# A one-core hybrid decoder layer: first products, broadcasts and gate rows in split passes

## The chip, the cores and the metric

One NeuronCore of a Trainium2 chip runs the whole layer as one program. The metric is device microseconds of one execution, the median of several runs.

## The reference, cut to what matters

One decoder layer over 512 tokens of width 2048, batch 1, float32. `c` gives shift, scale and gate through one matrix; the normed input goes through one wide input projection whose columns feed two head groups.

```
mod = silu(c) @ w_ada + b_ada;  shift, scale, gate = split(mod, 3)
h = rmsnorm(x, ln_g) * (1 + scale) + shift
p = h @ w_in + b_in
y_m = mlstm_group(...)      # 4 heads of 256, causal, chunkwise, gates i and f
y_n = nsa_group(...)        # 16 query heads, 4 groups of keys and values
y = concat(y_m, y_n) @ w_out
out = rmsnorm(x + gate * y, final_g)
```

In the second group, keys and values are also compressed: blocks of 32 tokens, 16 apart (31 blocks, 4 groups), are flattened to 2048 numbers and sent through `gelu(blk @ w1) @ w2` to a key and a value of 64 numbers each. Every query attends to the 31 compressed blocks, to selected blocks and to a window, and the three results are mixed by gates. In the first group the decay between two tokens needs one row per head, `fl - mr` (the running sum of the log forget gate less the running maximum), on all partitions. `gate` multiplies the rows of the output, so each of its 2048 numbers is needed on all partitions too.

## The kernel before, in words

Tokens lie on the free axis (512 columns), features on partitions, until the output projection. Almost every product is made of three TensorE passes on rounded operands (type F32R in the program): high by high, high by low and low by high, where `split` (L119) makes the high part with a copy on ScalarE (L123) and the low part with a subtraction (L126) on VectorE or, in the stretch where `pat` is "p", on GpSimd. `proj(name)` (L279) makes one tile of 128 input-projection columns: two loads of 512 KB into the tag `raw` (three buffers, L111), four quarters each split into tags `whi` and `wlo` (four buffers each), 48 matmuls of 512 columns (L291 to L293).

A few small products are still done on plain F32 operands, and each such call stands in the trace as two matmul records:

- `compress(kv)` (L437): the hidden layer of the compressed blocks, 16 calls for keys and 16 for values, the weights `raw` as the stationary operand and the gathered rows `cst`, read with a step of eight numbers, as the moving one (L444); then gelu and the second matrix.
- `memory_head` (L709): one row on 128 partitions, four partitions deep.
- `gate_columns` (L793): four column sums for each quarter of the gate.
- `chunk_rows` (L838): the gate columns turned to rows on all partitions, one 128-wide call for each.

In `gather` (L539) the weights of the 32 compressed blocks are transposed, split to `ph` and `pl`, and multiplied in two passes with `vcmp` (L548, L549), on 32 partitions; the same function serves the other two branches on 128 partitions.

The program is written in one order; a planner then orders the instructions of each engine by that order and by when buffers and inputs come free in its own reckoning, and gives out the buffers of a tag in the same way. Loads all go through one queue, SP's. Around the change the written order is: the projections kc0, kc1, vc0, then `compress(0)`, vc1, k0 and v0 for the first group, `compress(1)`, then the query tiles.

Of the kernel before, what the change touches and what calls it, by code (L numbers as in the profile page):

```python
# [10 lines left out]
F32 = mybir.dt.float32  # L11
F32R = mybir.dt.float32r
AF = mybir.ActivationFunctionType
# [73 lines left out]
def layer_kernel(ctx: ExitStack, tc: tile.TileContext, x, cols, ada, ada_g, w_ko, w_tiles,  # L87
# [18 lines left out]
    def psb(tag, name):  # L106
        return psum.tile([P, 512], F32, tag=tag, name=name, bufs=PSB[tag])
# [5 lines left out]
    def raw_tile(name):  # L113
        return ws.tile([P, 1024], F32, tag="raw", name=name, bufs=RAW)
# [164 lines left out]
    def proj(name, tag="pj"):  # L279

        ti = TIDX[name] - NKO
        ps = psb(tag, f"pj_{name}")
        for hf in range(2):
            raw = raw_tile(f"w_{name}_{hf}")
            nc.sync.dma_start(raw, w_tiles[ti, hf])
            for q in range(2):
                wh, wl = split(raw[:, q * 512:(q + 1) * 512], 512, f"w_{name}_{hf}{q}")
                for j in range(4):
                    k = hf * 8 + q * 4 + j
                    c = slice(j * P, (j + 1) * P)  # L290
                    pe.matmul(ps, wh[:, c], hhi[k], start=(k == 0), stop=False)  # L291
                    pe.matmul(ps, wh[:, c], hlo[k], start=False, stop=False)  # L292
                    pe.matmul(ps, wl[:, c], hhi[k], start=False, stop=(k == KT - 1))  # L293
# [6 lines left out]
    SIDE = 2  # L300

# [7 lines left out]
    gr = const.tile([P, T], F32, name="gr")  # L309
    kcmp = const.tile([P, NG, 32], F32, name="kcmp")  # L310
    vcmp = const.tile([32, NG, P], F32R, name="vcmp")
# [14 lines left out]
    na = napool.__enter__()  # L326

# [54 lines left out]
    rw = gr[64:68, :]  # L382
# [10 lines left out]
    ve.tensor_sub(rw, fl, mr)  # L393
# [17 lines left out]
    for hd in range(MH):  # L411
# [4 lines left out]
    cst = [[na.tile([P, 1056], F32, tag=("kh", "kl")[vr], name=f"cst{kv}{vr}", bufs=2)[:, :1024]  # L416
            .rearrange("p (g t) -> p g t", g=NG) for vr in range(2)] for kv in range(2)]
    def block_rows(kv, ct2):
        nm = f"{'kv'[kv]}c{ct2}"
        ps = proj(nm)  # L420
        for gg in range(2):
            r = slice(64 * gg, 64 * gg + 64)
            pv = ps[r, :].rearrange("p (b l r) -> p b l r", l=8, r=2)
            for par in range(2):
                for vr in range(2):
                    po = COLS["pos"][0] + ((kv * 2 + par) * 2 + vr) * 8
                    ve.scalar_tensor_tensor(
                        cst[kv][vr][64 * par:64 * par + 64, 2 * ct2 + gg, :]
                        .rearrange("p (b l) -> p b l", l=8),
                        pv[:, :, :, par], bcol(nm)[r, :],  # L430
                        ct[r, po:po + 8].unsqueeze(1).to_broadcast([64, 32, 8]),
                        op0=ALU.add, op1=ALU.add)

    gp.memset(kcmp, 0.0)
    ve.tensor_copy(vcmp.rearrange("p g c -> p (g c)"),
                   zero[0:32, 0:1].to_broadcast([32, NG * P]))
    def compress(kv):  # L437

        hid = psb("ms", f"hid{kv}")
        for half in range(2):  # L440
            raw = raw_tile(f"w1_{kv}{half}")
# [6 lines left out]
        hs = na.tile([P, NG * NCMP], F32, tag="hs", name=f"hs{kv}", bufs=1)  # L448
        sc.activation(hs, hid[:, 0:NG * NCMP], AF.Gelu_apprx_tanh)
        if kv == 0:  # L450
            kc = psb("ms", "kcps")
            pe.matmul(kc[:, 0:NG * NCMP], w2s[:, 0:128], hs, start=True, stop=True)
            ve.tensor_copy(kcmp[:, :, 0:NCMP],
                           kc[:, 0:NG * NCMP].rearrange("p (g b) -> p g b", b=NCMP))
        else:
            vc = psb("ms", "vcps")
            for g in range(NG):
                pe.matmul(vc[0:NCMP, g * DH:(g + 1) * DH], hs[:, g * NCMP:(g + 1) * NCMP],
                          w2s[:, 128:192], start=True, stop=True)
            vv = vc[0:NCMP, 0:NG * DH].rearrange("p (g d) -> p g d", d=DH)  # L460
            sc.copy(vcmp[0:NCMP, :, 0:DH], vv)
            ve.tensor_sub(vcmp[0:NCMP, :, DH:P], vv, vcmp[0:NCMP, :, 0:DH].bitcast(F32))

    block_rows(0, 0)
    block_rows(0, 1)
    block_rows(1, 0)
    compress(0)
    block_rows(1, 1)

    def kv_prep(g):  # L470
        kh = na.tile([P, 1056], F32R, tag="kh", name=f"kh{g}", bufs=2)
        kl = na.tile([P, 1056], F32R, tag="kl", name=f"kl{g}", bufs=2)
        sc.copy(kh[:, 0:32], kcmp[:, g, :])
        ve.tensor_sub(kl[:, 0:32], kcmp[:, g, :], kh[:, 0:32].bitcast(F32))
        ps = proj(f"k{g}")
# [23 lines left out]
    def attend(g, qs, kh, kl, vt):  # L499
# [6 lines left out]
        for i in reversed(range(NT)):  # L506
# [32 lines left out]
            def gather(srcs, rows, vmat, last, nme):  # L539

                tp = psb("tp", f"tp{nme}")
                for hd in range(HPG):
                    pe.transpose(tp[0:rows, hd * P:(hd + 1) * P], srcs[hd], ident)  # L543
                ph = na.tile([P, T], F32R, tag="ph", name=f"ph{nme}", bufs=2)
                pl = na.tile([P, T], F32R, tag="pl", name=f"pl{nme}", bufs=2)
# [63 lines left out]
    def state(g):  # L609
        kv = kv_prep(g)  # L610
        if g == 0:
            compress(1)
        return (q_prep(g), *kv)
# [54 lines left out]
    def memory_head(hd, vh, vl):  # L668
# [39 lines left out]
        dc = COLS["delta"][0] + hd * 16  # L708
        pe.matmul(rb, ct[64:68, dc:dc + 1].to_broadcast([4, P]), rw, start=True, stop=True)  # L709
# [68 lines left out]
    def gate_columns():  # L778
        for n in range(4):
            acc = na.tile([P, T], F32, tag="q", name=f"gacc{n}", bufs=QB)  # L780
            for k in range(KT):
# [12 lines left out]
            ve.tensor_add(gcol[:, 4 * n:4 * n + 4], ps[:, 0:4], col("b_agate", 4 * n, 4))  # L794
# [37 lines left out]
    wl_l = op.tile([P, KT, 256], F32R, name="wl_l")  # L832
    def chunk_rows(n, c0, cn):

        ps = psb("ms", f"gps{n}")
        for j in range(cn // P):
            k = c0 // P + j
            pe.matmul(ps[:, j * P:(j + 1) * P], gcol[:, k:k + 1].to_broadcast([P, P]), ident,  # L838
                      start=True, stop=True)
# [189 lines left out]
```

## Time and profile before

| | |
|---|---|
| median of 3 runs | 1138.44 us (1138.37 to 1139.06) |
| the profiled execution | 1138.83 us, span of its instructions 1137.0 us |
| TensorE matmul busy | 1110.3 us, 98% of the span |
| VectorE, ScalarE, GpSimd busy | 668.1, 546.6, 198.3 us |
| mean granted TensorE clock | 0.996 of full speed |

A matmul's record goes on for a while after the next one has begun, so the cost of one on a busy TensorE is read from its start to the start of the next, not from its length. In a timeline, rows that follow one another with the same operation and operands are merged, with their count behind x.

### The profile page before, as it was taken

Reading aid. Unit: us, or ns where it says so; the run is one execution under the profiler, and the core shown is the slowest. Engines: PE = TensorE matmul, PEld = TensorE weight load, DVE = VectorE, ACT = ScalarE, POOL = GpSimd, SP = SyncE. Lnnn points to the kernel's source line nnn. Section 1 sums busy time; section 2 is a strip of 40 time slices with the busy share of each in tenths; the row PEclk is TensorE's granted clock in tenths of the full one; section 3 lists DMA queues with packets and bytes.
Section 4 is the critical chain, followed back from the end, with each engine's and each line's share of the span. In section 5 each row is a group of like instructions: output and inputs, shape, how many; then the busy total and the mean of one; then the engine's idle time right before and its main releaser. Section 6 shows DMA issues by size and latency. Waiting matters only on the chain.

```text
span 1137.0 us, 18337 instructions
## 1 busy us (share of the span) xinstructions
PE 1110.3 (98%) x6796; PEld 919.1 (81%) x6796; DVE 668.1 (59%) x1712; ACT 546.6 (48%) x1222; POOL 198.3 (17%) x174
## 2 busy tenths in 40 slices
PE   4999999999999999999999999999999999999997
PEld 4777788887887888788788777888888888888896
DVE  5766464216647657666666885578567357334273
ACT  5443452237666758766756734333433354223242
POOL 1000200443335325333533210000000000000000
PEclk9999999999999999999999999999999999999999
DMA  9999423232111211121121442238416222444334
GB/s 378 406 402 363 146 93 130 93 112 74 56 56 59 72 56 56 62 68 57 61 70 57 138 158 77 91 134 290 151 57 214 84 91 75 148 140 133 104 114 158
DMA packets 49338, 150.29 MB, mean 132 GB/s; under 512 B 5856, under 2 KB 7776, under 8 KB 48736
## 3 DMA queue, kind: packets, MB, share of 16 engines
q1 hardware_dynamic: 49248, 149.12, 37.7%
q8 instruction: 53, 0.87, 0.3%
q14 instruction: 37, 0.30, 0.1%
HBM read 144.90 MB, written 4.19 MB: 131 GB/s over the span
## 4 chain that ended last, share of the span: by engine, by line
PE 93%; DVE 2%; DMA 2%; ACT 1%; issue 0%; POOL 0%; SPq 0%; ACTq 0%; POOLq 0%; DVEq 0%
PE ko L256 7%; PE po L899 5%; PE po L900 5%; PE po L901 5%; PE pj_q L291 3%; PE pj_mz L291 3%; PE pj_mx L291 3%; PE pj_mz L292 3%; PE pj_mv L291 3%; PE pj_q L292 3%; PE pj_mz L293 3%; PE pj_q L293 3%; PE pj_mx L292 3%; PE pj_mv L293 3%; PE pj_mv L292 3%; PE pj_mx L293 3%
## 5 line engine op out<-in xcount | busy, mean ns | idle before, releaser
L524 ACT ACTIVATE ep<-ep,nm 128x512 f32<-128x512 f32 (+3 forms) x128 | 71.3, 558 | 19.3 <-DVE nm L517 18.6
L749 POOL TENSOR_TENSOR sm<-sm,mhalf 128x1 f32<-128x1 f32 x16 | 10.1, 640 | 254.5 <-DVE sm L748 113.1
L788 DVE SCALAR_TENSOR_TENSOR gacc<-adag,sil,gacc 128x512 f32<-128x512 f32 x60 | 48.0, 801 | 7.5 <-DMA adag<-in_dram 6.9
L517 DVE CUSTOM_DVE_ANT_0 ep<-ss,bias 128x512 f32<-128x512 f32 (+3 forms) x64 | 30.3, 486 | 30.7 <-PE tps L543 22.1
L517 DVE CUSTOM_DVE_ANT_0 ep<-sw,bias 128x512 f32<-128x512 f32 (+3 forms) x64 | 29.9, 484 | 18.9 <-PE sw L585 12.9
L194 DVE SCALAR_TENSOR_TENSOR acc<-ada,sil,acc 128x256 f32<-128x256 f32 x75 | 35.7, 476 | 1.5
L220 ACT ACTIVATE hhi<-xts,md 128x512 fp32r<-128x512 f32 x16 | 13.1, 817 | 47.3 <-DVE md L210 47.3
L537 DVE TENSOR_SCALAR ep<-ep,ff 128x512 f32<-128x512 f32 (+3 forms) x80 | 33.2, 461 | 0.6
L861 POOL TENSOR_TENSOR rf<-rf,mhalf 128x1 f32<-128x1 f32 x4 | 2.2, 549 | 178.7 <-ACT tz L854 163.1
L547 DVE TENSOR_TENSOR pls<-tps,phs 128x512 fp32r<-128x512 f32 x40 | 27.0, 685 | 10.6 <-ACT phs L546 10.1
L547 DVE TENSOR_TENSOR plw<-tpw,phw 128x512 fp32r<-128x512 f32 x40 | 27.2, 684 | 6.7 <-ACT phw L546 6.1
L504 POOL TENSOR_SCALAR bias<-ct 128x640 f32<-128x640 f32 x16 | 29.4, 1839 | 2.3 <-DVE nm L517 1.2
L546 ACT CAST phw<-tpw 128x512 fp32r<-128x512 f32 x40 | 22.8, 583 | 13.3 <-PE tpw L543 8.4
L524 ACT ACTIVATE ec<-ec,nm 128x32 f32<-128x32 f32 x64 | 20.3, 317 | 17.6 <-DVE nm L517 17.2
L546 ACT CAST phs<-tps 128x512 fp32r<-128x512 f32 x40 | 23.0, 582 | 11.2 <-DVE nm L517 5.0
L203 PEld LDWEIGHTS gp<-ada,cb 128*32 128x32 f32 x1328 | 20.5, 112 | 8.9 <-issue 6.8
L543 PE MATMUL tpw<-ct,ep 128*128 128x128 f32 x160 | 26.8, 273 | 0.1
L517 DVE CUSTOM_DVE_ANT_0 ec<-ss,bias 128x32 f32<-128x32 f32 x48 | 8.9, 187 | 29.1 <-PE ss L575 28.8
L535 ACT ACTIVATE ep<-ep,ff 128x512 f32<-128x512 f32 (+3 forms) x48 | 23.5, 552 | 4.4 <-DVE ff L529 4.3
L232 PE MATMUL xt<-ct,xs 128*128 128x128 f32 x64 | 11.0, 330 | 14.3 <-DVE xs L169 12.4
L203 PE MATMUL gp<-ada,cb 128*32 128x64 f32 x1328 | 24.9, 224 | 0.0
L543 PE MATMUL tps<-ct,ep 128*128 128x128 f32 x160 | 24.8, 272 | 0.0
(1084 smaller groups left out, 3831.4 us busy)
## 6 DMA issues: line engine op xcount, KB each, us to landing
ada<-in_dram SPq DMA_DIRECT2D x64, 512.0 KB, 7.0
adag<-in_dram SPq DMA_DIRECT2D x64, 256.0 KB, 3.7
wo<-in_dram SPq DMA_DIRECT2D x32, 512.0 KB, 3.4
w_q<-in_dram SPq DMA_DIRECT2D x16, 512.0 KB, 3.5
w_mx<-in_dram SPq DMA_DIRECT2D x16, 512.0 KB, 3.4
w_mv<-in_dram SPq DMA_DIRECT2D x16, 512.0 KB, 3.4
w_mz<-in_dram SPq DMA_DIRECT2D x16, 512.0 KB, 3.5
w_mo<-in_dram SPq DMA_DIRECT2D x16, 512.0 KB, 3.4
```

The lines of the kernel that those rows point to most:

```text
L256: pe.matmul(ko_ps[j], (wl if p == 1 else wh)[:, c], (hlo if p == 2 else hhi)[k], start=(k == 0 and p == 0), stop=(k == KT - 1 and p == 2))
L291: pe.matmul(ps, wh[:, c], hhi[k], start=(k == 0), stop=False)
L292: pe.matmul(ps, wh[:, c], hlo[k], start=False, stop=False)
L293: pe.matmul(ps, wl[:, c], hhi[k], start=False, stop=(k == KT - 1))
L517: ve.tensor_tensor_reduce(dst, src, bs, -0.125, 3.0e38, ALU.add, ALU.min, nm[:, c:c + 1])
L524: sc.activation(tiles[hd], tiles[hd], AF.Exp, bias=nm[:, 4 * br + hd:4 * br + hd + 1], scale=-1.0, accum_out=zz[:, 4 * br + hd:4 * br + hd ...
L543: pe.transpose(tp[0:rows, hd * P:(hd + 1) * P], srcs[hd], ident)
L547: ve.tensor_sub(pl[0:rows, :], tp[0:rows, :], ph[0:rows, :].bitcast(F32))
L788: ve.scalar_tensor_tensor(acc, raw, w, acc, op0=ALU.mult, op1=ALU.add)
L899: pe.matmul(pss[i][:, :cn], yh[k][:, t], wh[:, c], start=f0, stop=False)
L900: pe.matmul(pss[i][:, :cn], yh[k][:, t], wl[:, c], start=False, stop=False)
L901: pe.matmul(pss[i][:, :cn], yl[k][:, t], wh[:, c], start=False, stop=l0)
```

## The change

It has five parts.

1. The hidden layer of the compressed blocks: `block_rows` now leaves rounded high and low rows (`csh`, `csl`), `w1` is split as well, into a tile `wt` that takes a buffer of the tag `raw`, and the operands change places: the rows are the stationary operand, the two halves of a weight stand side by side as 256 moving columns. A second call of 128 columns adds the low rows. The result has blocks on partitions, so it is transposed back (`compress_turn`). The steps are hung behind given projections: `turn(0)` behind vc1, the second layer of the keys and the values' hidden layer behind k0, `turn(1)` behind v0, the values' second layer behind the first query tile.
2. The row broadcast in `memory_head`: the row is split into eight partitions (high on four, low on four, carried there by a DMA from SBUF to SBUF) and multiplied in one pass.
3. `gather` for the compressed branch: high and low stand on 64 partitions of one tile, `vcmp` holds its rows twice, and one pass does both.
4. The gate columns: four calls on 32 columns of the array each, then a transpose on VectorE.
5. The gate rows: the columns are split, set on a diagonal by VectorE, and summed by a matrix of ones in two passes as wide as the chunk.

```diff
+        if name in behind:
+            with tc.issue_after(last):
+                behind[name]()
...
-    gr = const.tile([P, T], F32, name="gr")
+    rw = const.tile([8, T], F32R, name="rw")
+    dsel = const.tile([8, 64], F32R, name="dsel")
...
-    ve.tensor_sub(rw, fl, mr)
+    ve.tensor_copy(dsel, ds)
+    ve.tensor_sub(rd, fl, mr)
+    sc.copy(rh, rd)
+    ve.tensor_copy(rs[0:4, :], rh.bitcast(F32))
+    ve.tensor_sub(rd, rd, rh.bitcast(F32))
+    nc.sync.dma_start(rs[4:8, :], rd)
+    sc.copy(rw, rs)
...
+            ch, cl = cst[kv][vr]
+            c = slice(ct2 * 512, (ct2 + 1) * 512)
+            sc.copy(ch[:, c], cf)
+            ve.tensor_sub(cl[:, c], cf, ch[:, c].bitcast(F32))
...
+            def rows(t, l):
+                return t.rearrange("p (b l) -> p b l", l=8)[:, half:half + nb, l]
...
-            for l in range(8):
-                pe.matmul(hid[:, 0:NG * NCMP], raw[:, l * P:(l + 1) * P],
-                          cst[kv][half].rearrange("p g (b l) -> p g b l", l=8)
-                          [:, :, half:half + NCMP, l],
-                          start=(half == 0 and l == 0), stop=(half == 1 and l == 7))
+            for q in range(2):
+                rv = raw[:, q * 512:(q + 1) * 512]
+                wt = ws.tile([P, 2, 512], F32R, tag="raw", name=f"w1s{kv}{half}{q}", bufs=RAW)
+                sc.copy(wt[:, 0], rv)
+                ve.tensor_sub(wt[:, 1], rv, wt[:, 0].bitcast(F32))
+                for j in range(4):
...
+                    pe.matmul(hid[0:nb, 0:256].rearrange("p (v c) -> p v c", v=2), rows(ch, l), wt[:, :, c],
+                              start=f0, stop=False)
+                    pe.matmul(hid[0:nb, 0:P], rows(cl, l), wt[:, 0, c],
+                              start=False, stop=(half == 1 and l == 7))
...
+    def keys():
+        compress(0, hid[0])
+        hid[1] = compress_hidden(1)
+    behind.update(vc1=lambda: turn(0), k0=keys, v0=lambda: turn(1), q0_0=lambda: compress(1, hid[1]))
...
+                if rows == 32:
+                    sc.copy(ph[0:32, :], tp[0:32, :])
+                    ve.tensor_sub(ph[32:64, :], tp[0:32, :], ph[0:32, :].bitcast(F32))
+                    pe.matmul(ops, vmat, ph[0:64, :], start=first[0], stop=last)
...
-        pe.matmul(rb, ct[64:68, dc:dc + 1].to_broadcast([4, P]), rw, start=True, stop=True)
+        pe.matmul(rb, dsel[:, hd * 16:hd * 16 + 1].to_broadcast([8, P]), rw, start=True, stop=True)
...
-            for j in range(4):
-                pe.matmul(ps[:, j:j + 1], acc[:, j * P:(j + 1) * P], ones[:, 0:1], start=True, stop=True)
+            for g in range(4):
+                pe.matmul(ps[32 * g:32 * g + 32, 0:P].rearrange("p (j c) -> p j c", j=4), ones[:, 0:32],
+                          acc.rearrange("p (j c) -> p j c", j=4)[:, :, 32 * g:32 * g + 32],
+                          start=True, stop=True, tile_position=(0, 32 * g))
...
-            pe.matmul(ps[:, j * P:(j + 1) * P], gcol[:, k:k + 1].to_broadcast([P, P]), ident,
-                      start=True, stop=True)
+            dg = op.tile([P, 4, P], F32R, tag="dg", name=f"dg{n}{v}", bufs=2)
...
+            pe.matmul(ps[:, :cn], onr, dg[:, 0:m].rearrange("p a b -> p (a b)"), start=(v == 0), stop=(v == 1))
```

## Rows read from the trace of the kernel before

**Rows 1.** The page, busy time of each engine: us, share of the span, instructions.

```profile
PE 1110.3 (98%) x6796; PEld 919.1 (81%) x6796; DVE 668.1 (59%) x1712; ACT 546.6 (48%) x1222; POOL 198.3 (17%) x174
```

**Rows 2.** The page, shares of the chain that ended last.

```profile
PE 93%; DVE 2%; DMA 2%; ACT 1%; issue 0%; POOL 0%; SPq 0%; ACTq 0%; POOLq 0%; DVEq 0%
```

**Rows 3.** Stretches from:to: length, busy us per engine, granted clock, DMA share, GB/s.

```profile
130.00:262.00 132.00, 132.00 (x594) 109.57 (x594) 44.87 (x96) 49.62 (x82) 33.99 (x28) 1.00 0.31 103
...
637.30:640.70 3.40, 3.40 (x16) 3.10 (x16) 3.40 (x13) 3.40 (x10) 0.00 (x0) 0.50 0.50 169
```

**Rows 4.** Timeline of TensorE around the keys' hidden layer: start, length, operands, count.

```profile
184.98 0.39 PE L293 MATMUL pj_vc<-hhi,w_vc_11l 128*128 128x512 f32 x1
185.21 7.37 PE L444 MATMUL hid<-cst,w 128*128 128x124 f32 x32
192.22 0.60 PE L291 MATMUL pj_vc<-hhi,w_vc_00h 128*128 128x512 f32 x1
```

**Rows 5.** Timeline of TensorE: rounded operands, 128 and 256 moving columns.

```profile
828.16 0.27 PE L723 MATMUL s<-qh,xh 128*128 128x128 f32 x1
828.27 0.27 PE L724 MATMUL s<-ql,xh 128*128 128x128 f32 x1
...
1118.70 0.28 PE L908 MATMUL po<-wl_h,yh 128*128 128x256 f32 x1
1118.82 0.28 PE L909 MATMUL po<-wl_l,yh 128*128 128x256 f32 x1
```

**Rows 6.** Timeline of TensorE: passes on 32 partitions, one alone and a pair.

```profile
277.98 0.50 PE L548 MATMUL o<-phc,vcmp 32*128 32x512 f32 x1
278.40 0.50 PE L292 MATMUL pj_v<-hlo,w_v_10h 128*128 128x512 f32 x1
278.74 0.39 PE L293 MATMUL pj_v<-hhi,w_v_10l 128*128 128x512 f32 x1
...
656.25 0.49 PE L548 MATMUL o<-phc,vcmp 32*128 32x512 f32 x1
656.58 0.39 PE L549 MATMUL o<-plc,vcmp 32*128 32x512 f32 x1
656.90 0.50 PE L548 MATMUL o<-phs,v 128*128 128x512 f32 x1
```

**Rows 7.** Timeline of TensorE: the row broadcast of the first head.

```profile
563.99 1.12 PE L709 MATMUL rb<-gr,ct 4*128 4x512 f32 x2
565.04 0.50 PE L584 MATMUL sw<-kh,q_q 128*128 128x512 f32 x1
```

**Rows 8.** Timeline of TensorE: gate columns, and the sums on 32 columns of the array.

```profile
121.08 0.88 PE L203 MATMUL gp<-ada,cb 128*32 128x64 f32 x48
...
740.21 0.72 PE L793 MATMUL gcps<-ones,gacc 128*128 128x1 f32 x6
```

**Rows 9.** Timeline of TensorE: the gate rows of the first chunk.

```profile
947.10 1.05 PE L838 MATMUL gps<-ct,gcol 128*128 128x128 f32 x8
947.90 0.48 PE L899 MATMUL po<-wo000h,yh 128*128 128x512 f32 x1
```

**Rows 10.** Timeline of SP's queue: loads of `w1` for the keys, then the next projections.

```profile
170.18 1.98 SPq L442 DMA_DIRECT2D w<-in_dram  x2
178.85 5.82 SPq L285 DMA_DIRECT2D w_vc<-in_dram  x2
```

**Rows 11.** Instructions of `split`: length in ns (min/median/max) of copy and subtraction, by engine.

```profile
L123 ACT CAST w_q_00h<-w_q x8: 604/620/620, 220.1 to 431.1; 128x512 fp32r<-128x512 f32 x8
...
L126 DVE TENSOR_TENSOR w_mv_00l<-w_mv,w_mv_00h x6: 673/692/693, 674.7 to 870.2; 128x512 fp32r<-128x512 f32 x6
L126 POOL TENSOR_TENSOR w_k_00l<-w_k,w_k_00h x4: 1292/1296/1297, 195.9 to 378.4; 128x512 fp32r<-128x512 f32 x4
```

**Rows 12.** DMA issues: count, KB each, median us from issue to landing.

```profile
w_vc<-in_dram SPq DMA_DIRECT2D x4, 512.0 KB, 3.4
...
wg<-in_dram SPq DMA_DIRECT2D x4, 128.0 KB, 2.4
```

More of the change, by code (lines that the diff above doesn't have):

```diff
@@ L292, in proj @@
                     pe.matmul(ps, wh[:, c], hlo[k], start=False, stop=False)
-                    pe.matmul(ps, wl[:, c], hhi[k], start=False, stop=(k == KT - 1))
+                    last = pe.matmul(ps, wl[:, c], hhi[k], start=False, stop=(k == KT - 1)).ins
             if side_work:
@@ L300, in layer_kernel @@
     SIDE = 2
+    behind = {}
     def bcol(name):
@@ L326, in layer_kernel @@
     na = napool.__enter__()
+    gr = na.tile([P, T], F32, tag="q", name="gr", bufs=QB)
     def tmp(name, n=T):
@@ L392, in layer_kernel @@
     ve.tensor_tensor_scan(mr, fr, gr[0:4, :], 0.0, ALU.add, ALU.max)
-    ve.tensor_sub(rw, fl, mr)
+    rd = na.tile([P, T], F32, tag="q", name="rd", bufs=QB)[0:4, :]
+    rh = na.tile([P, T], F32R, tag="q", name="rh", bufs=QB)[0:4, :]
+    rs = na.tile([P, T], F32, tag="q", name="rs", bufs=QB)[0:8, :]
+    ds = na.tile([P, T], F32, tag="q", name="ds", bufs=QB)[0:8, 0:64]
+    for r in range(2):
+        nc.sync.dma_start(ds[4 * r:4 * r + 4, :], cols[0:4, COLS["delta"][0]:COLS["delta"][0] + 64])
+    ve.tensor_copy(dsel, ds)
[5 more added lines that the diff above has]
+    sc.copy(rw, rs)
     ve.tensor_sub(zt[0:4, :], gr[0:4, :], fl)
@@ L448, in compress @@
[L448 to L449 removed]
+            for q in range(2):
[4 more added lines that the diff above has]
+                for j in range(4):
+                    l = q * 4 + j
+                    c = slice(j * P, (j + 1) * P)
+                    f0 = half == 0 and l == 0
+                    pe.matmul(hid[0:nb, 0:256].rearrange("p (v c) -> p v c", v=2), rows(ch, l), wt[:, :, c],
+                              start=f0, stop=False)
+                    pe.matmul(hid[0:nb, 0:P], rows(cl, l), wt[:, 0, c],
+                              start=False, stop=(half == 1 and l == 7))
@@ new lines, in compress_hidden, with compress_turn, compress @@
+        hn = tmp(f"hn_{kv}", P)[0:nb, :]
+        sc.copy(hn, hid[0:nb, P:2 * P])
+        ve.tensor_add(hn, hn, hid[0:nb, 0:P])
+        sc.activation(hn, hn, AF.Gelu_apprx_tanh)
+        return hn
+    def compress_turn(kv, hn):
+        nb = NG * 32 - 1
+        hps = psb("ms", f"hsps{kv}")
+        pe.transpose(hps[:, 0:nb], hn, ident[0:nb, 0:nb])
+        hs = tmp(f"hs{kv}", nb)
+        ve.tensor_copy(hs, hps[:, 0:nb])
+        return hs
+    def compress(kv, hs):
+        nb = NG * 32 - 1
@@ L457, in compress, with turn @@
             for g in range(NG):
-                pe.matmul(vc[0:NCMP, g * DH:(g + 1) * DH], hs[:, g * NCMP:(g + 1) * NCMP],
+                pe.matmul(vc[0:NCMP, g * DH:(g + 1) * DH], hs[:, g * 32:g * 32 + NCMP],
                           w2s[:, 128:192], start=True, stop=True)
             vv = vc[0:NCMP, 0:NG * DH].rearrange("p (g d) -> p g d", d=DH)
[L461 to L468, printed above, removed]
+            for r in (0, 32):
+                sc.copy(vcmp[r:r + NCMP, :, 0:DH], vv)
+            for r in (0, 32):
+                ve.tensor_sub(vcmp[r:r + NCMP, :, DH:P], vv, vcmp[0:NCMP, :, 0:DH].bitcast(F32))
+    block_rows(0, 0, proj("kc0"))
+    block_rows(0, 1, proj("kc1"))
+    ps_vc0 = proj("vc0")
+    hid = {0: compress_hidden(0)}
+    def turn(kv):
+        hid[kv] = compress_turn(kv, hid[kv])
+    def keys():
+        compress(0, hid[0])
+        hid[1] = compress_hidden(1)
+    behind.update(vc1=lambda: turn(0), k0=keys, v0=lambda: turn(1), q0_0=lambda: compress(1, hid[1]))
+    ps_vc1 = proj("vc1")
+    block_rows(1, 0, ps_vc0)
+    block_rows(1, 1, ps_vc1)
     def kv_prep(g):
@@ L832, in layer_kernel @@
     wl_l = op.tile([P, KT, 256], F32R, name="wl_l")
+    gch = op.tile([P, KT], F32R, name="gch")
+    gcl = op.tile([P, KT], F32R, name="gcl")
+    onr = op.tile([P, P], F32R, name="onr")
+    sc.copy(gch, gcol)
+    ve.tensor_sub(gcl, gcol, gch.bitcast(F32))
+    sc.copy(onr, ones)
     def chunk_rows(n, c0, cn):
         ps = psb("ms", f"gps{n}")
-        for j in range(cn // P):
-            k = c0 // P + j
-            pe.matmul(ps[:, j * P:(j + 1) * P], gcol[:, k:k + 1].to_broadcast([P, P]), ident,
-                      start=True, stop=True)
+        m = cn // P
+        for v, gc in enumerate((gch, gcl)):
+            dg = op.tile([P, 4, P], F32R, tag="dg", name=f"dg{n}{v}", bufs=2)
+            ve.tensor_mul(dg[:, 0:m], ident.unsqueeze(1).to_broadcast([P, m, P]),
+                          gc[:, c0 // P:c0 // P + m].bitcast(F32).unsqueeze(2).to_broadcast([P, m, P]))
+            pe.matmul(ps[:, :cn], onr, dg[:, 0:m].rearrange("p a b -> p (a b)"), start=(v == 0), stop=(v == 1))
         gb = op.tile([P, 512], F32, tag="gb", name=f"gb{n}", bufs=2)
```

48 lines of the change are left out of this document (26 added, 22 removed).

## The prediction, made before the result was known

> **What bounds the kernel now.** I read the page's busy times first: TensorE is at a matmul for 1110.3 of 1137.0 us [rows 1], and the chain that ended last is 93% TensorE, 2% each VectorE and DMA [rows 2]. The busy times by stretch say the same of the place where most of the change lies: from 130 to 262 us TensorE is busy for all 132.00 us, VectorE for 44.87 and ScalarE for 49.62 [rows 3]. So a pass taken off TensorE's queue is worth its full place in that queue, as long as nothing makes the queue wait, and work added on VectorE or ScalarE is free as long as it comes in time. The price of a pass is the distance to the next start: a 512-column pass on rounded operands takes 0.23 us (184.98 to 185.21) [rows 4]. Five terms follow, then what the change puts in TensorE's way.
>
> **Hidden layer.** The keys' 16 calls are 32 records from 185.21 to 192.22, that is 7.01 us or 0.22 us a record, and the first pass behind them has a record of 0.60 us where its neighbours have 0.39, so 0.2 more is lost: 7.2 us [rows 4]. The gate rows, also plain F32 and with 128 moving columns side by side, take 0.10 us a record (947.10 to 947.90, eight) [rows 9]. The hidden layer's moving operand is read with a step of eight numbers, so I put the doubled price down to that step. After the change a call has 256 moving columns and another 128, all side by side, at 0.12 and 0.11 us [rows 5]: 16 x 0.23 = 3.7 us. Gain 3.5 us, twice: **7.0 us**.
> The step does not vanish, though: the rows are now the stationary operand, still read with a step of eight, and before shows no such weight load. Side by side, 128 columns load in at most the 0.11 us of rows 5, one number in 0.9 ns. The stepped moving operand costs 0.22 us for 124 columns [rows 4] in a record which, side by side, runs at 0.10 us [rows 9]. If stepped weights were slowed as much, each of the 32 loads would take 0.22 us and set the pace: 32 x 0.22 = 7.0 us, a gain of nothing. So this term lies between 0 and 7.0. I take 7.0, because rows 5 show 256 rounded columns in 0.12 us, about 0.5 ns a number, and 128 weights in 0.11: the weight load is already at half the pace of the moving read, and a step that only halves a read need not show in it.
> The Trainium skill, page "SBUF — State Buffer", section "Specifications (TRN2)", says full bandwidth needs at least two hits in a 16-byte line and each move to a new line is penalised. The doubled price of the stepped moving operand agrees; applied to the stationary one it speaks against this change, and is the second rival.
>
> **Compressed gather.** There are 16. In a pair the two passes on 32 partitions take 0.33 and 0.32 us (656.25, 656.58, 656.90); one alone takes 0.42 (277.98 to 278.40), and the pass behind it 0.34 instead of 0.23 [rows 6]. Fewer partitions cost a detour in and out, once per group of such passes. With 64 partitions I expect one alone, 0.42 for 0.65, so 0.23 us; 15 gathers stand as pairs (one of them here), 3.5 us, and the first is split over two places and saves 0.42 + 0.11 = 0.53: **4.0 us**. If 64 partitions had no detour, each pass would cost 0.23 us and each gather save 0.65 + 0.11 - 0.23 = 0.53 us at least, 8.5 in all; if one such pass cost 0.5, 2.7.
> The Trainium skill, page "TensorEngine Tiling (Array Packing)", section "Key Properties", says that a change of tiling mode drains the engine, and the page counts 64 rows as a mode of its own; by that it is 4.0 and not 8.5.
>
> **Row broadcast.** Two records per head hold TensorE from 563.99 to 565.04, 1.05 us [rows 7]. One rounded pass on eight partitions is again one alone, 0.42 [rows 6]: 4 x 0.63 = **2.5 us**.
>
> **Gate columns.** Six records take 0.72 us with the tail of the last; without it about 0.094 each, eight per quarter make 0.75 [rows 8]. The column-grouped sums of the ada product run 48 records of 64 columns in 0.88 us, 0.018 each [rows 8]; eight of twice the width are 0.29, and 0.1 for the change of form: 0.35 x 4 = **1.4 us** (0 to 2).
>
> **Gate rows.** 0.80 us for eight records [rows 9], 32 in all: 3.2 us. After: two passes per chunk, 0.23 for the three wide and 0.12 for the two narrow ones [rows 4, 5]: 1.9. **1.3 us**. The ten products on the diagonal are added on VectorE, 0.7 us each by the subtraction's length [rows 11], in the last 190 us, where the output pass over 16 tiles hides them. Without that cover each chunk would lose 1.4 us.
>
> **Added on TensorE.** Two transposes, 0.1 each [rows 9] and 0.2 for the pass behind [rows 4]: 0.6 us. Sum of the passes: 7.0 + 4.0 + 2.5 + 1.4 + 1.3 - 0.6 = **15.6 us** gained.
>
> **Waits that the change adds.** The row broadcast now has a DMA that waits in SP's queue for the row, with the loads of `w1` (170.18) [rows 10] behind it, and a copy on ScalarE that waits for its landing, about 2.4 us by the smallest load I list [rows 12], with splits behind it. Quarters split ahead hide both: four of them are 4 x 12 x 0.23 = 11 us of TensorE's work. I cost them at nothing; without that cover, 2 to 3 us once.
> The other one is not hidden. `wt` takes its buffers from the three of `raw`, and is held until TensorE has used it. Before, `w1` was loaded at 170.18 and just after, and the next projection's half at 178.85, 6 us ahead of the product at 185.21 [rows 10, 4]. Now `wt` for two quarters and one loaded half fill all three buffers when the product begins. Count from its start, a quarter being 4 x 0.23 = 0.93 us. The third quarter's `wt` gets a buffer at 0.93, and copy 0.62 and subtraction 0.69 [rows 11] make it ready at 2.3; TensorE was done at 1.86 and waits 0.4. The fourth is ready at 3.25, and TensorE ends at 4.2. Only at 3.25 is the loaded half free for the next projection's weights: 3.4 us to land [rows 12] and 0.62 to copy make 7.35. TensorE stands for 3.1 us, and its queue holds only work that is written behind. With the first low half this is 3.8 us for the keys. For the values the kc product must first be copied out of the one accumulator that both use (0.6), and GpSimd's subtraction takes 1.29 instead of 0.69 [rows 11]: 5.1 us. Together **8.9 us** lost, from below 1 (the planner gives a buffer to the next projection earlier) to 12.
>
> **Sum.** 15.6 - 8.9 = 6.7 us. The profiled execution took 1138.83 with a span of 1137.0, 0.4 above the median 1138.44; the difference is taken from the median: **1131.7 us**.
>
> **The rivals.**
> The waits are covered. If one buffer of `raw` goes to the next projection before `wt` is filled, as the load at 178.85 did [rows 10], its quarters fill TensorE's gaps, and only the 0.6 us at the shared accumulator is left: 1138.4 - 15.6 + 0.6 = 1123.4. For it: the load was early by 6 us before. Against: `wt` is written earlier in the program than those weights.
> The stepped weight load is slow. The hidden layer gains nothing, 8.6 us are left, and with quarters of 1.8 us the waits are shorter: the next weights are ready at 9.05 against an end at 7.2, so about 2.1 and 3.3 us. 8.6 - 5.4 = 3.2: 1135.2.
> Slower than before: the ring of `raw` closes fully. If both halves of `w1` are loaded before the first split, as the two loads at 170.18 were [rows 10], only one buffer is left for `wt`; then quarters one to three come one after another, and each product costs about 1.4 us more in waits. Together with a slow weight load that is 8.3 us. In addition TensorE's clock can fall: from 637.30 to 640.70 it was granted 0.50, the lower level, 1.2 GHz [rows 3], which at each of the two products would cost 1.7 us. 8.3 + 3.4 = 11.7 against 8.6: 1141.5. It decides once the waits exceed the gain by 2.3 us.
> It does not do what it says: 64 partitions, eight partitions or column groups bring nothing (7.9 us of the gain gone) with the waits as forecast: about 1139.6, within what counts as the same.
>
> **How the numbers follow.** Forecast 0.45, covered 0.25, slow weight load 0.18, closed ring 0.07, no effect 0.05. Taken to be told from no change is a difference of over 0.2%, 2.3 us, so faster is below 1136.2 and slower above 1140.7. Faster: 0.44 + 0.25 + 0.13 = 0.82. Same: 0.01 of the forecast, 0.05 of the third, 0.04 of the last: 0.10. Slower: 0.07 and 0.01. The range reaches from the covered case, 1122, to just past the slow load, 1136.5.
>
> **What would show it.** In the profile after: 32 pairs of 256 and 128 columns in the two hidden layers, 0.23 us a pair (0.45 if stepped weights are slow); one pass of 64 partitions in each gather, 0.42 and not 0.23; one rounded pass per head for the row; TensorE's wait behind each hidden layer, ended by ScalarE's copy of vc1's and v0's first quarter, about 3 us each; and the rest of TensorE's queue unchanged. I am wrong if TensorE's idle time between 180 and 260 us is below 2 us, or if a new order elsewhere in its queue moves more than 3 us.

## The result, and the profile after

The changed kernel takes 1153.2 us in the median of four runs (1152.0 to 1157.11), the kernel before 1138.66 beside it: a ratio of 1.0133, 95% interval 1.0109 to 1.0158. It is slower by about 15 us; forecast was 7 us faster. The profiled execution took 1152.00 us, its span 1150.2.

The page of the changed kernel, busy times and the shares of the chain that ended last, against [rows 1] and [rows 2]:

```profile
PE 1110.1 (97%) x6756; PEld 917.6 (80%) x6756; DVE 693.9 (60%) x1751; ACT 557.7 (48%) x1245; POOL 197.4 (17%) x174
...
PE 91%; DVE 4%; ACT 2%; DMA 1%; issue 1%; POOL 0%; SPq 0%; ACTq 0%; POOLq 0%; DVEq 0%
```

TensorE's busy time is what it was (1110.1 against 1110.3), so nothing was saved there on balance, and the span is 13.2 us longer. Busy times by stretch of the changed kernel (columns as in [rows 3]), the same 132 us first, then three stretches in it:

```profile
130.00:262.00 132.00, 122.77 (x526) 101.59 (x524) 54.85 (x112) 52.27 (x88) 28.53 (x23) 0.92 0.27 91
191.96:198.78 6.82, 4.33 (x13) 3.53 (x14) 2.79 (x5) 3.93 (x7) 0.00 (x0) 0.50 0.71 250
212.44:215.85 3.41, 2.93 (x7) 2.38 (x8) 3.30 (x7) 1.24 (x2) 0.00 (x0) 0.50 0.00 0
229.50:239.74 10.24, 8.34 (x27) 6.94 (x28) 1.69 (x5) 3.61 (x9) 3.95 (x4) 0.50 0.48 165
```

Before, TensorE was busy for all 132.00 us at the full granted clock. Now it is idle for 9.2 us, and for 20.5 us it is granted 0.50, the 1.2 GHz level. What it waits for in 130 to 262 us (engine, tile, line, releaser: us in total, times, longest):

```profile
PE pj_k L291 <- DVE cf_vc L449: 4.4, 1, 4.4
PE pj_vc L291 <- ACT w_vc_00h L123: 2.5, 1, 2.5
PE pj_v L291 <- ACT w_v_00h L123: 1.7, 1, 1.7
PE hid L483 <- DVE kcmp L507: 0.5, 1, 0.5
PE pj_v L293 <- POOL w_v_00l L126: 0.2, 1, 0.2
```

The timeline of TensorE around the keys' product, against [rows 4]:

```profile
185.74 0.29 PE L483 MATMUL hid<-w1s,csh 128*127 128x256 f32 x1
...
186.05 0.46 PE L483 MATMUL hid<-w1s,csh 128*127 128x256 f32 x1
186.35 0.35 PE L485 MATMUL hid<-w1s,csl 128*127 128x128 f32 x1
186.54 0.46 PE L483 MATMUL hid<-w1s,csh 128*127 128x256 f32 x1
...
193.09 0.34 PE L485 MATMUL hid<-w1s,csl 128*127 128x128 f32 x1
195.91 0.80 PE L291 MATMUL pj_vc<-hhi,w_vc_00h 128*128 128x512 f32 x1 [2.48 <-ACT w_vc_00h L123]
...
198.94 0.40 PE L292 MATMUL pj_vc<-hlo,w_vc_00h 128*128 128x512 f32 x1
...
208.28 0.27 PE L496 MATMUL hsps<-ct,hn 127*128 127x127 f32 x1
212.92 0.76 PE L291 MATMUL pj_k<-hhi,w_k_00h 128*128 128x512 f32 x1 [4.37 <-DVE cf_vc L449]
```

and of its weight loads (the engine row PEld) in the same stretch:

```profile
186.21 0.34 PEld L485 LDWEIGHTS hid<-w1s,csl 128*127 128x127 f32 x1
186.46 0.33 PEld L483 LDWEIGHTS hid<-w1s,csh 128*127 128x127 f32 x1
```

A pair of passes takes 0.48 us (186.05 to 186.54), where 0.23 were forecast, so the 16 of a product make 7.65 us instead of the 7.2 of before. The stationary loads begin 0.23 to 0.25 us apart, whether 256 or 128 columns move behind them. Behind the product stands the wait for vc1's first quarter; the first seven passes of vc1 then take 3.03 us (195.91 to 198.94), where seven at the full clock take 1.6. And k0 waits 4.4 us for VectorE, which no step of the prediction had.

How far the changed kernel is behind the kernel before, read from the ends of the projections' last passes in both traces:

| end of | us later than before |
|---|---|
| vc0 | 0.5 |
| vc1 | 4.7 |
| k0 | 10.8 |
| q1, the end of the stage | 16.4 |
| v3, in attention | 11.7 |
| mo0, behind attention | 19.9 |
| the last instruction | 13.2 |

So the stage with the hidden layers costs 16 us, the first part of attention gains about 5 of them back, the rest of it and the handover to the memory heads take 8 again, and what follows gives 7 back. An end also moves when the planner puts other work ahead of it, so the rows in and behind attention are not waits alone.

The other passes are as short as forecast. Timeline of TensorE after, against [rows 6], [rows 7] and [rows 9]: a gather, a row broadcast, a gate row.

```profile
295.89 0.50 PE L613 MATMUL o<-phc,vcmp 64*128 64x512 f32 x1
296.32 0.51 PE L619 MATMUL o<-phs,v 128*128 128x512 f32 x1
...
575.49 0.49 PE L777 MATMUL rb<-rw,dsel 8*128 8x512 f32 x1
575.91 0.49 PE L613 MATMUL o<-phc,vcmp 64*128 64x512 f32 x1
...
986.11 0.39 PE L922 MATMUL gps<-dg,onr 128*128 128x512 f32 x1
986.34 0.40 PE L984 MATMUL po<-wo040h,yl 128*128 128x512 f32 x1
```

From start to start that is 0.43, 0.42 and 0.23 us. Summed over all of their kind, the 16 gathers fell from 10.7 to 6.8 us, the row broadcasts from 4.2 to 1.9 (and two waits of 0.3 behind them), gate columns from 3.1 to 1.8, gate rows from 3.1 to 1.9: 8.7 us less on TensorE, against 9.2 forecast for these four.

### The profile page after: what moved, and what is told of

It is laid out like the page before. It is cut to its first block, busy times and chain, and to the rows that moved or that the text cites. A ratio compares the mean times of both kernels' runs of the same rounds, so it can differ in the third digit from the quotient of the medians.

```text
span 1150.2 us, 18308 instructions
## 1 busy us (share of the span) xinstructions
PE 1110.1 (97%) x6756; PEld 917.6 (80%) x6756; DVE 693.9 (60%) x1751; ACT 557.7 (48%) x1245; POOL 197.4 (17%) x174
## 4 chain that ended last, share of the span: by engine, by line
PE 91%; DVE 4%; ACT 2%; DMA 1%; issue 1%; POOL 0%; SPq 0%; ACTq 0%; POOLq 0%; DVEq 0%
PE ko L256 7%; PE po L982 4%; PE po L983 4%; PE po L984 4%; PE pj_mx L291 3%; PE pj_q L292 3%; PE pj_q L293 3%; PE pj_mv L291 3%; PE pj_q L291 3%; PE pj_mx L292 3%; PE pj_mv L293 3%; PE pj_mx L293 3%; PE pj_mv L292 3%; PE pj_mz L291 2%; PE pj_mz L293 2%; PE pj_mz L292 2%
## 5 line engine op out<-in xcount | busy, mean ns | idle before, releaser
L582 DVE CUSTOM_DVE_ANT_0 ep<-sw,bias 128x512 f32<-128x512 f32 (+3 forms) x64 | 29.9, 485 | 21.5 <-PE sw L656 13.7
L203 PEld LDWEIGHTS gp<-ada,cb 128*32 128x32 f32 x1328 | 20.5, 112 | 9.1 <-issue 6.9
L608 PEld LDWEIGHTS tps<-ct,ep 128*128 128x128 f32 x160 | 20.2, 142 | 5.3 <-PE sw L656 0.5
```

The lines of the kernel that those rows point to most:

```text
L582: ve.tensor_tensor_reduce(dst, src, bs, -0.125, 3.0e38, ALU.add, ALU.min, nm[:, c:c + 1])
```

## The experiments

**The change cut in two.** First the hidden layer alone (part 1, the rest as before), then parts 2 to 5 alone.

> Only the first part of the change (the split hidden layer of the compressed blocks with its order behind the projections); gather, row broadcast, gate columns and gate rows as before. Theory A, the loss lies in the compressed stage: in the profile of the changed kernel that stage ends 15.9 us later than before, so this should take 1138.7 + 15.9 = about 1154.5 us. Theory B, the loss comes from the new order of everything behind that stage: about 1141 us, with TensorE's waits between 180 and 260 us much shorter than the 9.3 us of the changed kernel.

Measured 1156.4 us, a ratio of 1.0144 (1.0129 to 1.0159). The waits and the half clock are those of the changed kernel: 4.4 us ahead of k0, 2.5 ahead of vc1, 1.9 and 0.5 around the values' product, and a granted clock of 0.50 for 20.5 us of the stage. The loss is part 1's.

> The other four parts without the first. Theory A: faster than before. By the sum of the prediction (4.0 + 2.5 + 1.4 + 1.3) 9.2 us, so 1129.5 us; by what the changed kernel shows behind the compressed stage, only 2.7 us, so 1136 us. Theory B: slower than before, about 1148 us.

Measured 1139.0 us, 0.9994 (0.9984 to 1.0003): no difference. It is 4.7 us ahead of the kernel before at the end of mz1 and 5.8 behind at the end of mo0, with 0.50 granted for 6.8 us there. In the changed kernel these parts do give something: it is 16.4 us behind at the end of the stage and 13.2 at its last instruction. Where the gain goes comes back below.

**The order of the block rows.** In the changed kernel:

```diff
-    ps_vc1 = proj("vc1")
     block_rows(1, 0, ps_vc0)
+    ps_vc1 = proj("vc1")
```

> The changed kernel with one line moved: the block rows of vc0 stand in the program ahead of the projection vc1 and its transpose, not behind. Theory A, k0's first pass waits 4.4 us because VectorE reaches the block rows of vc0 only behind the copy of the transposed hidden layer: the wait goes, and with it the stretch of half clock at 212.4 to 215.8: 4 to 6 us less, about 1148 us. Rival: k0 waits for its weights or for another buffer as well: the wait moves and the time stays at 1153 us.

Measured 1148.3 us, 1.0073 (1.0058 to 1.0088), 5 us below the changed kernel; the wait ahead of k0 is gone. The half clock that theory A let go with it stayed: 6.8 us from 191.6 on and 13.7 from 222.3 on, 20.5 in the stage as in the changed kernel. VectorE's timeline in the changed kernel shows where it came from:

```profile
205.48 0.69 DVE L478 TENSOR_TENSOR w1s<-w,w1s 128x512 fp32r<-128x512 f32 x1 [7.09 <-ACT w1s L477]
208.59 0.29 DVE L498 COPY hs<-hsps 128x127 f32<-128x127 f32 x1 [2.42 <-PE hsps L496]
208.80 5.48 DVE L449 SCALAR_TENSOR_TENSOR cf_vc<-pj_vc,ct 64x256 f32<-64x256 f32 x11
```

The block rows of vc0 (L449) could have been read from 185.9 us on, when vc0 ended, and VectorE stood idle for most of 198.4 to 208.6. But they stood in its queue behind the copy of the transposed hidden layer (L498), and that waits for a transpose which TensorE makes only behind vc1. `proj` has two accumulators, and vc0's is k0's.

**The step of the stationary load.** The block rows are written so that the stationary operand of a pass lies side by side; everything else as in the changed kernel:

```diff
-    ...cf[64 * par:64 * par + 64, gg * 256:(gg + 1) * 256].rearrange("p (b l) -> p b l", l=8),
+    ...cf[64 * par:64 * par + 64, :].rearrange("p (l b) -> p b l", l=8)[:, gg * 32:(gg + 1) * 32, :],
```

> The changed kernel with the block rows stored so that the 127 numbers of one stationary load lie side by side; the products are the same. Theory A, the step of eight numbers doubles the weight load: a pair of passes takes 0.24 us instead of 0.48, the two products 7.6 us less together, and half of that comes back as longer waits for the buffers of the loads: 1146 to 1150 us. Rival, loads of rounded weights take 0.24 us here for another reason: pairs stay at 0.48 us and the time at 1153 us.

Measured 1158.0 us, 1.0164 (1.0147 to 1.0181): the pairs fell to 0.23 us, as the theory says, 8 us less in the two products, and the kernel was 5 us slower still. What TensorE waits for in 130 to 262 us in this kernel, the four longest:

```profile
PE pj_k L291 <- DVE cf_vc L449: 5.7, 1, 5.7
PE hid L484 <- DVE w1s L479: 3.4, 2, 2.3
PE pj_vc L291 <- ACT w_vc_00h L123: 2.7, 1, 2.7
PE pj_v L291 <- ACT w_v_00h L123: 2.3, 1, 2.3
```

and VectorE's block rows in it (length in ns, min/median/max, then first and last start):

```profile
L449 DVE SCALAR_TENSOR_TENSOR cf_vc<-pj_vc,ct x16: 641/662/690, 210.3 to 223.0; 64x256 f32<-64x256 f32 x16
```

The step had moved to VectorE's writes, which now stand 64 numbers apart and take 0.66 us each instead of 0.48, in front of the accumulator that k0 waits for. The shorter product also ran into its own quarters (3.4 us), a wait of the kind that the prediction had worked out for short passes, and 23.9 us were granted at 0.50. So the price of the step was shown, and what it is worth was not: the waits had to go first.

**Rows first, and the split weights out of the ring.** `wt` takes buffers of a tag that attention uses later:

```diff
-            for q in range(2):
-                rv = raw[:, q * 512:(q + 1) * 512]
-                wt = ws.tile([P, 2, 512], F32R, tag="raw", name=f"w1s{kv}{half}{q}", bufs=RAW)
+            for q in range(4):
+                rv = raw[:, q * 256:(q + 1) * 256]
+                wt = na.tile([P, 2, 256], F32R, tag="ep", name=f"w1s{kv}{half}{q}", bufs=8)
```

> The changed kernel with two repairs: the block rows of vc0 stand ahead of the projection vc1, and the split quarters of the hidden layer's weights lie in buffers that attention uses later, so that no projection's weights wait for them in the ring of raw weights (they are split in eighths of 256 columns for that). The hidden products keep the stepped weight load. Compared with the kernel that has the first repair alone (1148.3 us). Theory A (the waits bring the half clock behind them): the idle time ahead of vc1 and v0, 1.6 and 1.8 us, goes, and with it the half clock in these projections, some 3 us each: about 1139 to 1141. Theory B (the hidden products themselves bring the half clock, being bound by the weight load): the 3.4 us of waits go and the half clock of 13.7 us stays: about 1145. Theory C (the eighths come too late, since ScalarE and VectorE now split twice as many pieces): the waits move to the hidden products and the time stays near 1148.

Measured 1141.4 us, 1.0019 (1.0010 to 1.0029), 6.9 us below the kernel with the rows first alone, just above the upper edge of theory A. No wait longer than 0.3 us is left in the stage. But the half clock did not go with the waits. Two stretches of this kernel, the first ending where the clock falls inside the keys' product:

```profile
186.20:191.79 5.59, 5.59 (x26) 5.47 (x24) 4.33 (x9) 1.14 (x2) 0.00 (x0) 1.00 0.81 283
191.79:198.60 6.81, 6.81 (x22) 5.90 (x22) 3.85 (x10) 2.10 (x7) 0.00 (x0) 0.50 0.09 34
```

TensorE was busy without a gap ahead of the fall, from 187.02 on with pairs on the stepped load. In the side-by-side kernel the clock fell at 193.80, behind a wait of 2.3 us in the product. In the changed kernel two of the three falls came inside a hidden product with TensorE in no wait (191.96 and 229.50), and one in the wait ahead of k0 (212.44). So both went ahead of a fall here, and neither theory has it alone.

**And the block rows turned.** VectorE's 16 writes stay; the copy and the subtraction that split a block read with the step instead:

```diff
-            c = slice(ct2 * 512, (ct2 + 1) * 512)
-            sc.copy(ch[:, c], cf)
-            ve.tensor_sub(cl[:, c], cf, ch[:, c].bitcast(F32))
+            cv = cf.rearrange("p (b l) -> p l b", l=8)
+            hv, lv = [t.rearrange("p (l b) -> p l b", l=8)[:, :, ct2 * 64:(ct2 + 1) * 64] for t in (ch, cl)]
+            sc.copy(hv, cv)
+            ve.tensor_sub(lv, cv, hv.bitcast(F32))
```

> As the kernel with the rows first and the split weights out of the ring, and in addition the block rows are turned when they are split into hi and lo: the 8 VectorE writes of a block stay as they are, and ScalarE's copy and VectorE's subtraction of 512 columns read with a step and write so that a stationary load of the hidden product is contiguous. Theory A (the step alone doubles the load, and only VectorE's scattered 8 writes made the side-by-side kernel slow): a pair of passes is 0.23 us instead of 0.48, each product is some 4 us shorter, 8 us in all against the kernel without the turn: 1131 to 1137. Theory B (a stream of short passes with waits around it falls to half clock again, as in the side-by-side kernel with 24 us at half): 1140 to 1147, with more half clock than without the turn.

Measured 1132.2 us, 0.9936 (0.9920 to 0.9952): 9.2 us below the kernel without the turn. The stage in this kernel:

```profile
130.00:262.00 132.00, 130.86 (x619) 107.60 (x618) 71.94 (x142) 68.02 (x123) 38.33 (x29) 1.00 0.33 105
```

and ScalarE's copies with the step (ns, min/median/max; the median is 621 in the changed kernel):

```profile
L457 ACT CAST csh<-cf_kc x4: 1150/1176/1192, 169.3 to 184.5; 128x512 fp32r<-128x512 f32 x4
```

Clock 1.00 all through the stage, 1.1 us idle. The step costs the copy 0.56 us a block, on an engine that has time for it; VectorE's subtraction takes 1.14 us for the keys and 1.57 (1.15 to 2.11) for the values instead of 0.69, and why the values take more was not looked into.

**The operand of the kernel before.** There the same step lay on the moving operand. Here `cst` is stored the other way round, and the full-precision products stay:

```diff
-                          cst[kv][half].rearrange("p g (b l) -> p g b l", l=8)
-                          [:, :, half:half + NCMP, l],
+                          cst[kv][half].rearrange("p l (g b) -> p l g b", g=NG)
+                          [:, l, :, half:half + NCMP],
```

> The kernel before, with one thing changed: the block rows are stored so that the moving operand of a hidden product's pass is contiguous (it was read with a step of 8 numbers). The products stay 16 passes of full precision, no split, no extra load of the ring. Theory A (a step of 8 numbers costs the moving operand as it costs the stationary one): each of a pass's two records goes from 0.22 us to 0.11, a product from 7.2 to 3.7 us, the time falls by about 7 us: 1131 to 1134. Theory B (0.22 us is what a record of 124 columns costs here whatever the step): the records stay 0.22 and the time stays at 1139, or rises by up to 3 us, since VectorE's 8 writes of a block now take 0.69 us each instead of 0.50.

Measured 1132.2 us, 0.9935 (0.9919 to 0.9950). Timeline of TensorE in this kernel, against [rows 4]:

```profile
185.84 3.73 PE L444 MATMUL hid<-cst,w 128*128 128x124 f32 x32
189.33 0.48 PE L291 MATMUL pj_vc<-hhi,w_vc_00h 128*128 128x512 f32 x1
```

32 records in 3.49 us, 0.11 each instead of 0.22. VectorE's writes are 0.67 us here too and hold nothing up. The whole gain that the split was to bring lay in how the operand is stored: no split, no second load, no ring.

**Where parts 2 to 5 lose their gain.** On that kernel, parts 2 to 5 in addition:

> The kernel with parts 2 to 5 of the change alone (gather on 64 rows, row broadcast, gate columns, gate rows; 1139.0 us), and the contiguous moving operand in the unsplit hidden products. Theory A (the operand's step doubles the price of a hidden pass): 7 us less than that kernel, 1130 to 1133, and the stretch where attention hands over to the memory heads still gives back some 4 us of what the parts gain. Theory B (the step costs nothing): 1139 to 1141.

Measured 1132.9 us, 0.9942 (0.9924 to 0.9959): again nothing from these parts, 11.5 us ahead at mz1 and 1.3 at mo0. VectorE was busy for 38.3 of the 40 us from 630 to 670, so its gate accumulations were taken out of that stretch:

```diff
         if hd == 0:
             pat[0] = "v"
+        if hd == 1:
             side_work.append(gate_columns())
```

> The kernel with parts 2 to 5 alone and the contiguous moving operand (1132.9 us), with one line moved: the gate columns' accumulation on VectorE starts one memory head later. In that kernel the parts were 11.5 us ahead of the kernel before at the projection mz1 and 1.3 us ahead at mo0, and between 630 and 670 us VectorE was busy 38.3 of 40 us, 16.1 of it with 18 of these accumulations. Theory A (the gain is given back because VectorE has no time left in that stretch): without the accumulations VectorE has some 16 us of room there, the waits of 2.0, 1.7 and 0.7 us and part of the half clock go, and 4 to 8 us come back: 1125 to 1129. Theory B (the gain is given back to the chain from the last attention tile over the first memory head, whatever VectorE does beside it): within 2 us of 1132.9. Rival on the other side: the accumulations are late at the end, where the output needs them: over 1135.

> The same line moved in the kernel before with the contiguous moving operand (1132.2 us), without parts 2 to 5. Theory A: this kernel too loses 2 to 5 us where attention hands over (at mz1 it is 6.7 us ahead of the kernel before, at mo0 5.5, and it has waits of 0.4 to 0.9 us there), so that it gains 1 to 4 us: 1128 to 1131; the kernel with parts 2 to 5 and the same move is then 3 to 5 us faster than this one, which is what these parts are worth when nothing takes it back. Theory B: 1131 to 1133, and no difference between the two.

> The same line moved in the wholly repaired change (rows first, split weights out of the ring, block rows turned while split; 1132.2 us). At mz1 it was 9.3 us ahead of the kernel before and at mo0 0.0. Theory A: 5 to 9 us come back: 1123 to 1128, level with the kernel of parts 2 to 5 with the unsplit products, since a split product of contiguous passes (7.4 us in the profile for both on TensorE) costs what the unsplit one costs. Theory B: within 2 us of 1132.2.

Measured 1128.5 with parts 2 to 5 (0.9899, 0.9882 to 0.9915), 1129.6 without them (0.9915, 0.9900 to 0.9930), and 1130.2 for the repaired change (0.9919, 0.9904 to 0.9934). The move is worth 2.1 to 4.5 us, but VectorE was not the cause of the loss ahead of mo0: now busy for 27.8 of the 40 us in the first of the three, it left that kernel only 1.9 us ahead at mo0. The first was 1.1 us faster than the second, where 3 to 5 were expected, and the third missed its expectation by 2 us. All kernels with the gather had one thing that those without it lacked, a wait of 2.0 us ahead of a gather of the window branch. So the parts were taken apart once more, on the kernel without them:

> The kernel before with the contiguous moving operand and the late gate accumulations (1129.6 us), and of the change only the row broadcast, the gate columns and the gate rows, no gather on 64 rows. Theory A (the gather brings the loss at the handover with it): there is neither the 2.0 us wait nor half clock between 600 and 700 us, and the shorter passes pay, some 1.0 to 1.8 us for the broadcasts and 2.0 to 2.6 for the gates: 1125.0 to 1127.0, faster than with the gather too (1128.5). Theory B (the broadcasts and gates stand beside other work and pay nothing): 1129 to 1130.

> The same base (1129.6 us) and of the change only the gather on 64 rows. Theory A: at the projection mz1 it is some 4 us ahead of its base, and it gives all of it back at the handover, with the 2.0 us wait ahead of the gather of the window branch and 3 to 7 us of half clock: 1129 to 1132. Theory B (the gather pays and something else in parts 2 to 5 takes it back): 1125.5 to 1127.

Measured 1126.0 us for row broadcast and gates without the gather (0.9884, 0.9869 to 0.9899), the fastest kernel here, and 1131.8 for the gather alone (0.9931, 0.9918 to 0.9943), 2.3 slower than its base. Added to the kernel with row broadcast and gates, the gather costs 2.5 us (1126.0 to 1128.5). A stretch of the kernel with the gather alone:

```profile
635.50:642.30 6.80, 5.66 (x17) 4.25 (x16) 6.13 (x11) 4.46 (x15) 4.53 (x3) 0.55 0.23 77
```

and the same of the kernel with row broadcast and gates alone:

```profile
635.50:642.30 6.80, 6.80 (x34) 5.57 (x33) 5.45 (x11) 4.44 (x14) 4.43 (x3) 1.00 0.25 77
```

TensorE's timeline tells what differs. With the gather alone:

```profile
631.68 0.60 PE L545 MATMUL tpc<-ct,ec 128*32 128x128 f32 x4
634.29 0.49 PE L556 MATMUL o<-phw,v 128*128 128x512 f32 x1 [2.00 <-ACT phw L554]
634.78 0.51 PE L710 MATMUL qk<-xh,ah 128*128 128x512 f32 x1
...
637.16 0.79 PE L293 MATMUL pj_mo<-hhi,w_mo_00l 128*128 128x512 f32 x1 [1.14 <-POOL w_mo_00l L126]
```

and in its base, without it:

```profile
633.83 0.51 PE L702 MATMUL qk<-xh,ah 128*128 128x512 f32 x1 [0.78 <-ACT ah L695]
...
636.33 0.50 PE L293 MATMUL pj_mo<-hhi,w_mo_00l 128*128 128x512 f32 x1 [0.86 <-POOL w_mo_00l L126]
...
639.19 0.39 PE L548 MATMUL o<-phw,v 128*128 128x512 f32 x1
```

and ScalarE's, first with the gather alone, then in the base:

```profile
633.65 0.58 ACT L554 CAST phw<-tpw 128x512 fp32r<-128x512 f32 x1
634.12 0.61 ACT L703 ACTIVATE ah<-wqk 128x512 fp32r<-128x512 f32 x1
...
633.18 0.59 ACT L695 ACTIVATE ah<-wqk 128x512 fp32r<-128x512 f32 x1
...
635.21 0.60 ACT L546 CAST phw<-tpw 128x512 fp32r<-128x512 f32 x1
```

In the base the pass on this tile's `phw` stands behind the first passes of `qk` and `pj_mo`, and ScalarE's copy, at 635.21, is long done when TensorE comes to it. With the shorter gathers the planner orders the queues anew, TensorE's and ScalarE's: that pass stands ahead of `qk` and its copy ahead of `ah`, which `qk` needs. The copy is even earlier, at 633.65, but TensorE has run out of work at 632.3 and waits for it, and `ah`, ready only at 634.73, could not have filled the wait. From 636.2 on, within a further wait of 1.1 us for GpSimd, it is granted 0.50 for 6.8 us.

The handover is not all. Between 420 and 600 us, in attention, the kernel with the gather alone has waits that its base does not have, 2.3 us in all, most of it for VectorE's low part of a gather of the window branch:

```profile
PE o L557 <- DVE plw L555: 1.9, 2, 1.0
```

An estimate of the whole: the gathers are 3.9 us shorter; against it stand these 2.3 us, 0.8 us more idle time between 600 and 670 (3.5 against 2.7), and 3.4 for 6.8 us at half clock, 2.6 us more than they save, where 2.3 were measured. The half clock does not come in every execution: two of five had a mean granted clock of 0.997 instead of 0.994 or 0.995, and took 1130.6 and 1130.7 us, still over a microsecond more than the base. That the gather brings the loss is shown; what the same gather would gain in the old order was not tried, and why the planner's order turns out so was not looked into.

## Why the prediction was wrong, step by step

**Hidden layer: 7.0 forecast, -0.9 measured.** This is the term that failed. Its bounds were 0 and 7.0 and I took the upper end, because "a step that only halves a read need not show" in a load that already runs at half the pace. It shows: loads of 127 columns follow one another every 0.24 us with the step and every 0.11 to 0.12 side by side (pairs of 0.48 and 0.23). The lower bound was too high as well, by 0.9 us. Both operands pay double for the step, 0.22 and 0.24 us, and both get it back when they lie side by side, as the kernel before with the contiguous operand and the repaired change show. The Trainium skill, page "SBUF — State Buffer", section "Specifications (TRN2)", which penalises each move to a new line, agrees with both rows. The second rival had the pair at 0.45 and the waits at 2.1 and 3.3 us (2.5 and 2.4 measured, with those at the shared accumulator and for GpSimd); it missed the time by the two terms that follow and by the gain of the other parts, which mostly did not come.

**A moved step and the queue it holds up: 0 forecast, 4.4 measured.** The prediction counted who waits for the ring, not what stands behind the moved transpose on VectorE: block rows that free k0's accumulator. One line moved takes it away.

**The clock: in a rival of 0.07, 5.0 us measured.** Seven passes each of vc1 and k0 and eight of v0 cost 1.4, 1.4 and 2.1 us more at the level of 1.2 GHz. The rival's 3.4 came from one stretch of before [rows 3] and had two falls, not three. Two of the three came inside the slow products, one in the wait ahead of k0.

**The ring: 8.9 forecast, 4.9 measured.** It is of the forecast kind and place; with passes twice as long the quarters come in time, as the second rival said. Of the 2.5 us behind the keys' product not all is the ring. ScalarE's timeline:

```profile
193.46 0.27 ACT L488 COPY hn<-hid 127x128 f32<-127x128 f32 x1 [3.25 <-PE hid L485]
193.75 1.28 ACT L490 ACT_TABLE_LOAD   x1
195.04 0.31 ACT L490 ACTIVATE hn<-hn 127x128 f32<-127x128 f32 x1
195.26 0.60 ACT L123 CAST w_vc_00h<-w_vc 128x512 fp32r<-128x512 f32 x1
```

The load of vc1's first half, issued at 190.97, is there at about 194.4 by its 3.5 us; the copy then still stands behind the gelu and the table that it loads, until 195.26. I had not put these on ScalarE's queue.

These four and the 0.6 forecast for the transposes make 0.9 + 4.4 + 5.0 + 4.9 + 0.6 = 15.8 of the 16.4 us at the end of the stage.

**Gather, row broadcast, gates: 9.2 forecast, 8.7 measured on TensorE, 0 to 3 in the time.** The durations were right, among them 0.42 for a pass on 64 partitions. In the changed kernel they give back 3.2 us behind the stage (16.4 to 13.2), beside the kernel before nothing (1139.0 against 1139.8), and with the contiguous operand nothing (1132.9 against 1132.2). The claim that failed is "the rest of TensorE's queue unchanged": the gather changes the order of everything behind it and gives back more than its gain, in waits in attention and in waits and half clock at the handover. Row broadcast and gates, with which the handover stays as it was, bring 3.5 us (1129.6 to 1126.0) of the 5.2 forecast for them.

**The sign that it would be wrong** held: "a new order elsewhere that moves more than 3 us" is what the table above shows between v3 and mo0. It does not name the largest miss; that has its own sign there, the pair at 0.45 if the load is slow (0.48 measured).

Together: 7.9 us for the hidden layer, 4.4 for the moved step, 5.0 for the clock and 6.0 of the other parts' gain that did not come, less 4.0 that the ring cost less than forecast, make 19.3 of the 20.3 us by which the profiled execution (1152.0) lies above the forecast (1131.7).

## What to carry to other kernels

Before splitting a product to make it cheaper, look at how its operands lie: a step of eight numbers doubled every pass, on either operand, and storing the rows side by side gained 6.8 us where the split alone lost 17. When a step is moved, list what stands behind it on every engine's queue, and which buffer that work frees. And where a planner orders the queues, a shorter pass can bring an order that costs more than it saves, as the gather's did; measure each part by itself and keep those that pay, as the row broadcast and the gates did.

## What the runs showed of the hardware

- A stationary load of rounded operands with a step of eight numbers sets the pace of its passes: in the changed kernel the loads begin every 0.23 to 0.25 us, whether 128 or 256 columns move; side by side the pair of 256 and 128 columns takes 0.23 us together.
- The same step costs ScalarE's copy of 512 columns 1.18 us instead of 0.62 when read, and VectorE's subtraction 1.14 (keys) and 1.57 (values) instead of 0.69 when read. VectorE's write of 256 columns takes 0.66 instead of 0.48 with a step of 64 numbers.
- The granted clock fell to 1.2 GHz in a product that ran without a gap on stepped loads (191.79 us, in the kernel with the rows first and the split weights out of the ring), and it stayed at 2.4 GHz through the same product side by side in the repaired change.
- On stepped loads the half clock itself cost nothing here: a pair takes 0.48 us at either level (186.05 to 186.54, and 192.27 to 192.75 in the changed kernel). The cost comes in the 512-column passes behind it, 0.43 us instead of 0.23 (seven from 195.91 to 198.94).
